# Moving the residual adds of two projections and two sets of weight sums from VectorE to GpSimd in a transformer layer kernel

## The chip, the cores and the metric

The kernel runs on one core of a Trainium2 chip. A core has TensorE (PE) for matrix products, VectorE (DVE), ScalarE (ACT) and GpSimd (POOL) for elementwise work, and SyncE (SP), which in this kernel issues nearly all transfers. Each engine executes its own queue of instructions. The metric is the device time of one execution in microseconds. The kernel before took 2554.41 us, the median of three runs (2552.43 to 2555.48).

## What is computed

One layer on x (2048 x 1024): token mixing (sliding-window attention and a gated linear recurrence, whose outputs are concatenated and projected by w_out), cross-attention with 4 heads into 256 memory tokens, and a dense SwiGLU FFN, each with a norm before and after and a residual. Cut to what matters here:

```python
y = jnp.concatenate([ya, yh], axis=-1) @ w_out[l]
h = h + rms_norm(y, g_mix_post[l])
u = rms_norm(h, g_x_pre[l])
m = rms_norm(mem, g_mem[l])
y = cross_attention(u, m, wq_x[l], wk_x[l], wv_x[l], wo_x[l])
h = h + rms_norm(y, g_x_post[l])
u = rms_norm(h, g_ffn_pre[l])
y = (jax.nn.silu(u @ w_gate[l]) * (u @ w_up[l])) @ w_down[l]
h = h + rms_norm(y, g_ffn_post[l])
```

All is float32.

## The kernel before

**Folded weights.** `fold_cross` makes, for each head, the products of the query weights with the memory's keys and of the memory's values with the output weights. They are stored as two matrices of 1024 x 1024, `qk_d` and `vo_d`. The scores are then one product of the tokens with `qk_d`, and the attention's output one product of the probabilities with `vo_d`.

**Precision.** Each float32 operand is split into a high part (ScalarE, or GpSimd in early stages, L987 and L989) and a low part, the difference (VectorE, L990). A product is three matmuls: L1131 high x high, L1132 high x low of T, L1133 low of S x high. S are the stationary tiles of a block, made anew for each (`streamed`, 5 buffers), T the moving ones of 512 columns, which stay for a whole job.

**Seven products for eight.** From the out projection on, the work is a list of jobs (`jobs`): out projection, scores, values, two halves of gate and up, three parts of the down projection. Each job multiplies a matrix, cut into 2 x 2 blocks, with 8 blocks of 256 tokens (22 of hidden rows) by Strassen's scheme in Winograd's form, seven steps of 12 matmuls a block in place of eight (`seven`). This needs sums of the blocks of both operands. S's sums are formed by VectorE for each block (L1106). T's sums are chains of four adds and subtractions, which `combined` (L1027 on) makes one job ahead: it loads two operands into tiles, combines them in place (L1034), and stores the result to HBM (L1035 calls `store`, on SP's queue). Each chain is done in two halves, thus 8 adds of 128 x 1024 for a job. The sums of `w_out` are made during token mixing, those of query-key (`qk_s`) beside the out projection, those of value-output (`vo_s`) beside the scores, the FFN's later (L1465 to L1473). A tile of the sums has few buffers: `extra` one, the second tile is a `row` (12 buffers, shared with the blocks' rows) for `qk_s` and a gain's tile for `vo_s`.

**The blocks.** `mixed_block` is the out projection of 256 tokens. Its `out` adds two PSUM or SBUF parts to a row y and squares it (L1526 on VectorE or L1528 on ScalarE, then L1504 on ScalarE). Its `after` works beside the following block's steps, a piece a step (each `yield` ends one): the norm's factors (`rstds`, three small GpSimd instructions, L1515 to L1519), y times factor and gain on VectorE (L1557), y plus the residual x (L1558), and the store of y to `h1_d`; then, two steps on, the squares of the new y on ScalarE, its norm's factors, and 32 x 32 transposes by VectorE (L1398) with a store for the score stage. `score_block` takes the maximum of each head's scores on VectorE (L1588), scales it on GpSimd (L1590) and forms exponentials on ScalarE (L1592). `value_block` scales y (L1630), adds the residual (L1634), stores it, squares it, scales it for the FFN (L1643) and transposes it on TensorE (L1390).

**Order.** `phases` goes through the steps: TensorE's products of a step, then the S tiles needed two steps on, then one piece of every follow-up and of the sums, then a split of the next job's T. On each engine the order of instructions is set at build by a simulated timeline. `behind` pins what is traced inside it behind the last ScalarE and VectorE instructions that were traced before (L1033); the pin holds for instructions on those two engines. SP's queue holds loads and stores in one order; a store that waits for its tile holds up the loads behind it.

Of the kernel before, what the change touches and what calls it, by code (L numbers as in the profile page):

```python
# [15 lines left out]
ALU = mybir.AluOpType  # L16
# [32 lines left out]
class Layer:  # L49
# [942 lines left out]
    CHAIN = (5, 7, 6, 4)  # L992

    def resident(self, get, nk, key, dst, keep, sums):


# [27 lines left out]
                keep[key] = src  # L1024
            yield lambda a=a, b=b, t=t, o=o: split(a, b, t, o)

    def combined(self, get, nk, dst):  # L1027

        nc = self.nc
        halves = [(0, (nk + 1) // 2), ((nk + 1) // 2, nk)]  # L1030
        for a, b in halves:
            def put(key, t, o, op):
                with self.behind():  # L1033
                    nc.vector.tensor_tensor(t, t, o, op)  # L1034
                self.store(dst[self.CHAIN.index(key), :, a * 512:b * 512], t.rearrange("p k d -> p (k d)"))  # L1035

            for x, y, key in (((0, 1), (0, 0), 5), ((1, 1), (0, 1), 7), (None, (0, 0), 6), (None, (1, 0), 4)):
                if x:
                    t = get(0, *x, a, b - a)
                o = get(1, *y, a, b - a)  # L1040
                for _ in range(3):
                    yield
                if key == 4:
                    put(4, o, t, ALU.subtract)
                else:
                    put(key, t, o, ALU.add if key == 6 else ALU.subtract)
                yield
# [132 lines left out]
    def plain(self, S, T, nk, out, keep, kind):  # L1180
# [36 lines left out]
        yield  # L1217

    def phases(self, jobs, first, prologue=None):


# [193 lines left out]
            p = P if i else 64  # L1415
            self.load(d, self.I["w_out"][r:r + p * n, j * 512:(j + 1) * 512].rearrange("(k p) d -> p k d", p=p))

    def sums(self, name, src, nk, *tiles):

        dst = self.tc.dram_tile([4, P, nk * 512], F32, name=name)  # L1420

        def get(which, i, j, k0, n):
            t = tiles[which]().rearrange("p (k d) -> p k d", d=512)[:, :n]
            src(t, i, j, k0, n)
            return t

        return dst, lambda: self.combined(get, nk, dst)

    def token_sums(self, a, o, n):

# [10 lines left out]
    def jobs(self):  # L1441
        I = self.I

        def weights(src, r0, nk):
            return lambda t, i, j, k0, n: self.load(
                t, src[r0 + (i * nk + k0) * P:r0 + (i * nk + k0 + n) * P, j * 512:(j + 1) * 512]
                .rearrange("(k p) d -> p k d", p=P))

        def ffn_u(b):
            return lambda t, i, j, k0, n: self.load(  # L1450
                t, self.u_d[4 * i + k0:4 * i + k0 + n, :, b * TB + j * 512:b * TB + (j + 1) * 512]
                .rearrange("k p t -> p k t"))

        def kinds(blocks, n=0, last="p"):
            return [("p" if i < n else last if i == len(blocks) - 1 else "s",) + b for i, b in enumerate(blocks)]

        def sums(name, src, nk, other=None):
            return self.sums(name, src, nk, self.extra_tile, other or self.gain_tile)

        def in_turn(*what):  # L1460
            return lambda: itertools.chain.from_iterable(w() for w in what)

        qk, vo = weights(self.qk_d, 0, 4), weights(self.vo_d, 0, 4)
        down = [(weights(I["w_down"], f0 * P, nk), f0, nk) for f0, nk in ((0, 3), (6, 4), (14, 4))]
        qk_s, vo_s = sums("qk_s", qk, 4, self.row_tile), sums("vo_s", vo, 4)  # L1465
        u_s = sums("u_s", ffn_u(1), 4)
        self.u0_s = self.tc.dram_tile([4, P, 4 * 512], F32, name="u0_s")
        d_s = [sums(f"d_s{c}", src, nk) for c, (src, _, nk) in enumerate(down)]
        jobs = [(self.w_out, 4, kinds([self.mixed_block(n) for n in range(0, NT, 2)], 1), self.out_sums, {1: [qk_s[1]]}),
                (qk, 4, kinds([self.score_block(n) for n in range(0, NT, 2)]), qk_s[0], {1: [vo_s[1]]}),  # L1470
                (vo, 4, kinds([self.value_block(n) for n in range(0, NT, 2)]), vo_s[0], {})]
        for b in range(NB):
            beside = {2: [in_turn(*(d[1] for d in d_s))]} if b else {4: [u_s[1]]}  # L1473
            jobs.append((ffn_u(b), 4, kinds([blk for f in range(0, NFF, 2) for blk in self.hidden_blocks(b, f)], 0, "s"),
                         u_s[0] if b else self.u0_s, beside))
        for c, (src, f0, nk) in enumerate(down):
            jobs.append((src, nk, kinds([self.down_block(c, f0, nk, n) for n in range(0, NT, 2)], 0, "s"), d_s[c][0], {}))

        return jobs
# [59 lines left out]
    def mixed_block(self, n):  # L1539
        nc = self.nc  # L1540
        y, x, ss = {}, [], []

        def out(i, j, a, b):
            if not y:
                x.extend(self.rows_of(self.I["x"], n + r) for r in range(2))
                ss.append(self.small("q_s", 4))
                if not n:
                    self.g_mix_post = self.gain(self.I["g_mix_post"])
            if i not in y:
                y[i] = self.row_tile()  # L1550
            self.squared(y[i][:, j * 512:(j + 1) * 512], a, b, ss[0][:, 2 * i + j:2 * i + j + 1])

        def after():
            r = self.rstds(ss[0])
            s2 = self.small("q_s", 4)
            for i in range(2):
                nc.vector.scalar_tensor_tensor(y[i], y[i], r[:, i:i + 1], self.g_mix_post, ALU.mult, ALU.mult)  # L1557
                nc.vector.tensor_tensor(y[i], y[i], x[i], ALU.add)  # L1558
                self.store(self.h1_d[(n + i) * P:(n + i + 1) * P, :], y[i])
                yield  # L1560
            yield
            for i in range(2):
                self.mean_squares(y[i], i, s2)
                yield
            r = self.rstds(s2)
            nc.gpsimd.tensor_scalar(self.r_x[:, n:n + 2], r, 1.0, None, ALU.mult)
            yield
            for i in range(2):
                self.store_blocked(self.h1t_d[n + i], self.blocked(y[i], self.row_tile()))
                yield  # L1570

        return self.tokens(self.y_d, n), out, after, None
# [37 lines left out]
    def value_block(self, n):  # L1610
        nc = self.nc
        y, ss, u, o = {}, [], {}, {}

        def out(i, j, a, b):
            if not y:
                ss.append(self.small("q_s", 4))
            if i not in y:
                y[i] = self.row_tile()
                if n == 0 and len(y) == 1:
                    self.g_x_post = self.gain(self.I["g_x_post"])  # L1620
                    self.g_ffn_pre = self.extra_tile()
                    self.load(self.g_ffn_pre, self.I["g_ffn_pre"][0:1, :].broadcast_to([P, D]))
            self.squared(y[i][:, j * 512:(j + 1) * 512], a, b, ss[0][:, 2 * i + j:2 * i + j + 1])

        def after():
            r = self.rstds(ss[0])
            s2 = self.small("q_s", 4)
            x = [self.rows_of(self.h1_d, n + i) for i in range(2)]
            for i in range(2):
                nc.vector.scalar_tensor_tensor(y[i], y[i], r[:, i:i + 1], self.g_x_post, ALU.mult, ALU.mult)  # L1630
            yield
            yield
            for i in range(2):
                nc.vector.tensor_tensor(y[i], y[i], x[i], ALU.add)  # L1634
                self.store((self.out if n < NT - 2 else self.h2_d)[(n + i) * P:(n + i + 1) * P, :], y[i])
                yield
            for i in range(2):
                self.mean_squares(y[i], i, s2)
                yield
            r = self.rstds(s2)  # L1640
            yield
            for i in range(2):
                nc.vector.scalar_tensor_tensor(y[i], y[i], r[:, i:i + 1], self.g_ffn_pre, ALU.mult, ALU.mult)  # L1643
                yield
            for i in range(2):
                u[i] = self.transposed(y[i], y[i])
                self.store_transposed(self.u_d, n + i, u[i])
                if 4 <= n < 8:
                    o[i] = self.row_tile().rearrange("p (k t) -> p k t", k=KT)
                    self.load(o[i], self.u_d[:, :, (n - 4 + i) * P:(n - 3 + i) * P].rearrange("k p t -> p k t"))  # L1650
                yield
            if o:
                yield
                for i in range(2):
                    yield from self.token_sums(u[i], o[i], n - 4 + i)

        return self.blocks(self.pt_d, n), out, after, None

    def hidden_blocks(self, b, f):
# [131 lines left out]
```

## Time and profile before

| | us |
|---|---|
| median of three runs | 2554.41 |
| the profiled execution | 2550.01 |
| its span, first to last instruction | 2548.3 |
| residual rows of the out projection (L1557), first to last start | 800.8 to 946.1 |
| maxima of the scores (L1590), first to last start | 962.7 to 1099.5 |
| residual rows of the values (L1634), first to last start | 1132.8 to 1289.2 |

The profile lists, for each engine, when an instruction ran, what it waited for and who waited for it. A row such as "L990 DVE TENSOR_TENSOR S<-sum,S 128x512" names the line of the kernel, the engine, the operation, the tile written and the tiles read, and the shape (partitions x elements). Idle time of an engine is put down to whatever ended it. Some matmul records are missing from a trace, so counts of matmuls can be a few per cent low. The granted TensorE clock was 0.997 of full speed.

The moved instructions are those of L1558 (16 times, 805.5 to 953.7 us), L1634 (16 times, 1132.8 to 1289.2), and of L1034 those of `qk_s` (8 times, 811.3 to 893.0) and `vo_s` (8 times, 982.4 to 1054.1).

### The profile page before, as it was taken

To read this page: it belongs to the slowest core of one execution; us is meant where nothing else is said; L and a number is where in the kernel's file an instruction comes from. 1 tells how busy PE (TensorE), PEld (TensorE's weight loads), DVE (VectorE), ACT (ScalarE), POOL (GpSimd) and SP (SyncE) were. 2 spreads that over 40 slices of the span, in tenths; PEclk is the share of its full clock that TensorE was granted. 3 is DMA by queue.
4 is the path that set the end of the run, shared out by engine and by line. 5 is a ranking of instruction groups with operands and counts; after the bars stand their busy time and mean duration, and the time that the engine had idled before them with its cause. 6 is when DMAs were issued, how large, how long until landed. Compare 5 with 4: busy or idle time off the path is not lost.

```text
span 2548.3 us, 34324 instructions
## 1 busy us (share of the span) xinstructions
PE 2504.8 (98%) x12006; PEld 2092.8 (82%) x12006; DVE 1792.1 (70%) x2871; ACT 1261.6 (50%) x2635; POOL 364.6 (14%) x540
## 2 busy tenths in 40 slices
PE   9999999999999999999999999999999999999998
PEld 8878888877997778878878888888888888878886
DVE  8885488987556989988876555576566557574766
ACT  5553466655555566566753333353333335443543
POOL 4231234321311112102200000000000000000022
PEclk9999999999999999999999999999999999999999
DMA  6455655865887996867954522254465434564786
GB/s 201 146 165 178 192 154 170 230 204 146 259 292 275 316 335 189 274 206 226 333 200 146 177 91 87 74 203 148 160 210 195 144 117 159 180 188 106 228 177 151
DMA packets 387885, 486.33 MB, mean 191 GB/s; under 512 B 22272, under 2 KB 283392, under 8 KB 387712
## 3 DMA queue, kind: packets, MB, share of 16 engines
q1 hardware_dynamic: 381664, 462.12, 55.9%
q0 software_dynamic: 6048, 22.02, 5.0%
q8 instruction: 94, 1.54, 0.2%
q14 instruction: 79, 0.65, 0.1%
HBM read 317.34 MB, written 166.72 MB: 190 GB/s over the span
## 4 chain that ended last, share of the span: by engine, by line
PE 51%; DVE 2%; DMA 1%; issue 1%; ACT 1%; POOL 0%; SPq 0%; DVEq 0%; POOLq 0%; ACTq 0%
PE psm L1133 17%; PE psm L1131 17%; PE psm L1132 17%; DVE T L990 0%; DVE S L990 0%; ACT junk L1504 0%; PE pss L1390 0%; DMA out_dram<-row 0%; DMA row<-d_s 0%; DMA row<-in_w_down_dram 0%; DMA u_d<-row 0%; DMA sraw<-in_w_gate_dram 0%; DVE sum L1106 0%; ACT S L987 0%; ACT T L987 0%
## 5 line engine op out<-in xcount | busy, mean ns | idle before, releaser
L1131 PE MATMUL psm<-T,S 128*128 128x512 f32 x2680 | 1034.1, 390 | 13.3 <-ACT part L1146 7.2
L1132 PE MATMUL psm<-T,S 128*128 128x512 f32 x2680 | 1042.3, 390 | 4.0 <-DVE T L990 3.9
L1133 PE MATMUL psm<-T,S 128*128 128x512 f32 x2680 | 1029.4, 389 | 4.1 <-DVE S L990 4.1
L1131 PEld LDWEIGHTS psm<-T,S 128*128 128x128 f32 x2680 | 503.0, 188 | 125.9 <-ACT part L1146 11.9
L1132 PEld LDWEIGHTS psm<-T,S 128*128 128x128 f32 x2680 | 503.2, 188 | 110.5 <-DVE T L990 7.3
L1133 PEld LDWEIGHTS psm<-T,S 128*128 128x128 f32 x2680 | 503.1, 188 | 110.6 <-DVE S L990 6.3
L987 ACT ACTIVATE S<-sum 128x512 fp32r<-128x512 f32 (+1 forms) x370 | 224.0, 620 | 371.5 <-PE psm L1133 267.3
L990 DVE TENSOR_TENSOR S<-sraw,S 128x512 fp32r<-128x512 f32 (+1 forms) x315 | 211.5, 679 | 218.8 <-ACT S L987 215.8
L1146 ACT ACTIVATE part<-psm 128x512 f32<-128x512 f32 x285 | 168.6, 596 | 251.9 <-PE psm L1133 230.9
L990 DVE TENSOR_TENSOR S<-sum,S 128x512 fp32r<-128x512 f32 (+1 forms) x388 | 257.4, 673 | 42.1 <-ACT S L987 38.3
L987 ACT ACTIVATE S<-sraw 128x512 fp32r<-128x512 f32 (+1 forms) x300 | 184.7, 618 | 110.8 <-PE psm L1133 106.0
L1537 POOL DMA_DIRECT2D y_d<-row x16 | 14.1, 879 | 1077.9 <-DVE row L1721 1027.6
L990 DVE TENSOR_TENSOR T<-row,T 128x1024 fp32r<-128x1024 f32 (+1 forms) x112 | 131.0, 1183 | 30.2 <-ACT T L987 29.2
L157 PE MATMUL psg<-u,whi 128*128 128x512 f32 x320 | 128.3, 401 | 0.0
L158 PE MATMUL psg<-u,wlo 128*128 128x512 f32 x320 | 127.6, 399 | 0.0
L156 PE MATMUL psg<-u,whi 128*128 128x512 f32 x320 | 127.5, 399 | 0.0
L1504 ACT ACTIVATE junk<-row 128x512 f32<-128x512 f32 x160 | 99.6, 624 | 40.6 <-DVE row L1526 20.6
L987 ACT ACTIVATE T<-row 128x1024 fp32r<-128x1024 f32 (+1 forms) x112 | 113.3, 1031 | 7.5 <-DMA row<-d_s 4.3
L1672 DVE TENSOR_TENSOR row<-psm,part 128x512 f32<-128x512 f32 x66 | 43.7, 687 | 66.9 <-PE psm L1133 66.9
L1681 DVE TENSOR_TENSOR part<-psm,part 128x512 f32<-128x512 f32 x66 | 43.8, 687 | 60.1 <-PE psm L1133 59.8
L1721 DVE TENSOR_TENSOR row<-psm,part 128x512 f32<-128x512 f32 x72 | 49.1, 688 | 49.5 <-PE psm L1133 49.4
L814 ACT ACTIVATE S<-S,w_mn 128x256 f32<-128x256 f32 (+1 forms) x128 | 63.0, 496 | 29.6 <-DVE w_mn L810 29.2
(363 smaller groups left out, 3562.2 us busy)
## 6 DMA issues: line engine op xcount, KB each, us to landing
sraw<-in_w_gate_dram SPq DMA_DIRECT2D x44, 512.0 KB, 3.6
sraw<-in_w_up_dram SPq DMA_DIRECT2D x44, 512.0 KB, 3.7
hid_d<-row SPq DMA_DIRECT2D x44, 512.0 KB, 2.7
sraw<-hid_d SPq DMA_DIRECT2D x32, 512.0 KB, 4.2
sraw<-in_w_in_dram SPq DMA_DIRECT2D x44, 256.0 KB, 4.0
z_d<-pair SPq DMA_DIRECT2D x20, 512.0 KB, 3.4
raw<-in_w_in_dram SPq DMA_DIRECT2D x20, 512.0 KB, 4.8
z_d<-z SPq DMA_DIRECT2D x20, 512.0 KB, 4.0
```

The source lines that it names most:

```text
L156: nc.tensor.matmul(ps, ah, bh, start=(i == 0), stop=False)
L157: nc.tensor.matmul(ps, ah, bl, start=False, stop=False)
L158: nc.tensor.matmul(ps, al, bh, start=False, stop=(i == n - 1))
L814: nc.scalar.activation(s[:, r, o:], s[:, r, o:], AF.Exp, bias=mn[:, i:i + 1], scale=-1.0, accum_out=den[:, i:i + 1])
L987: self.nc.scalar.activation(hi, raw, AF.Copy)
L990: self.nc.vector.tensor_tensor(lo, raw, f32(hi), ALU.subtract)
L1131: nc.tensor.matmul(ps, s[:, 0, k, :], t[:, 0, k, :], start=st, stop=False, **kw)
L1132: nc.tensor.matmul(ps, s[:, 0, k, :], t[:, 1, k, :], start=False, stop=False, **kw)
L1133: nc.tensor.matmul(ps, s[:, 1, k, :], t[:, 0, k, :], start=False, stop=sp, **kw)
L1146: nc.scalar.activation(t, ps, AF.Copy)
L1504: self.nc.scalar.activation(junk, a, AF.Square, scale=float(D) ** -0.5, accum_out=to)
L1721: nc.vector.tensor_tensor(d, a, b, ALU.add)
```

## The change

Two kinds of adds are issued on GpSimd in place of VectorE: the residual adds of `mixed_block` (L1558) and `value_block` (L1634), and the in-place adds of the sums `qk_s` and `vo_s` (L1034), through a new argument of `combined` and `sums`. The sums of `w_out`, of the FFN's tokens and of `w_down` stay on VectorE, as do all other instructions.

```diff
-    def combined(self, get, nk, dst):
-
-        nc = self.nc
+    def combined(self, get, nk, dst, on):
+
         halves = [(0, (nk + 1) // 2), ((nk + 1) // 2, nk)]
         for a, b in halves:
             def put(key, t, o, op):
                 with self.behind():
-                    nc.vector.tensor_tensor(t, t, o, op)
+                    on.tensor_tensor(t, t, o, op)
...
-    def sums(self, name, src, nk, *tiles):
+    def sums(self, name, src, nk, *tiles, on=None):
...
-        return dst, lambda: self.combined(get, nk, dst)
+        return dst, lambda: self.combined(get, nk, dst, on or self.nc.vector)
...
-        def sums(name, src, nk, other=None):
-            return self.sums(name, src, nk, self.extra_tile, other or self.gain_tile)
+        def sums(name, src, nk, other=None, **at):
+            return self.sums(name, src, nk, self.extra_tile, other or self.gain_tile, **at)
...
-        qk_s, vo_s = sums("qk_s", qk, 4, self.row_tile), sums("vo_s", vo, 4)
+        qk_s, vo_s = sums("qk_s", qk, 4, self.row_tile, on=self.nc.gpsimd), sums("vo_s", vo, 4, on=self.nc.gpsimd)
...
                 nc.vector.scalar_tensor_tensor(y[i], y[i], r[:, i:i + 1], self.g_mix_post, ALU.mult, ALU.mult)
-                nc.vector.tensor_tensor(y[i], y[i], x[i], ALU.add)
+                nc.gpsimd.tensor_tensor(y[i], y[i], x[i], ALU.add)
                 self.store(self.h1_d[(n + i) * P:(n + i + 1) * P, :], y[i])
...
             for i in range(2):
-                nc.vector.tensor_tensor(y[i], y[i], x[i], ALU.add)
+                nc.gpsimd.tensor_tensor(y[i], y[i], x[i], ALU.add)
                 self.store((self.out if n < NT - 2 else self.h2_d)[(n + i) * P:(n + i + 1) * P, :], y[i])
```

## The prediction

> **What bounds the kernel now.** I read the page's engine shares first, then the busy time by stretches, then who kept TensorE waiting, then single stretches of VectorE and GpSimd in order of time.
>
> ```profile
> span 2548.3 us, 34324 instructions
> PE 2504.8 (98%) x12006; PEld 2092.8 (82%) x12006; DVE 1792.1 (70%) x2871; ACT 1261.6 (50%) x2635; POOL 364.6 (14%) x540
> ```
>
> TensorE is the bound over the whole span: 2548.3 - 2504.8 = 43.5 us are all that can be gained anywhere. The edits lie in the three stages with folded cross-attention weights: out projection, scores, values. Here is the busy time of these (rows one to three) and of the following FFN stretch (row four):
>
> ```profile
> core 0: us, PE busy (x) PEld busy (x) DVE busy (x) ACT busy (x) POOL busy (x), PEclk, DMA share, GB/s
> 800.00:960.00 160.00, 153.24 (x666) 124.04 (x665) 143.69 (x184) 99.44 (x220) 25.61 (x50) 1.00 0.92 309
> 960.00:1120.00 160.00, 158.73 (x700) 130.90 (x699) 150.42 (x276) 99.35 (x227) 27.38 (x36) 1.00 0.77 235
> 1120.00:1320.00 200.00, 193.25 (x901) 157.24 (x900) 165.45 (x208) 128.59 (x275) 31.91 (x48) 1.00 0.76 251
> 1320.00:1700.00 380.00, 380.00 (x1678) 314.75 (x1677) 220.24 (x329) 144.25 (x249) 0.00 (x0) 1.00 0.39 129
> ```
>
> TensorE idles 6.76 us in the first stage, 1.27 in the second and 6.75 in the third, 14.8 in all; nothing in the FFN stretch. VectorE is busy 90%, 94% and 83% there. GpSimd is almost free by this count. Who ended TensorE's waits between 780 and 1320 us (sum, times, longest):
>
> ```profile
> PE psm L1133 <- DVE S L990: 4.1, 4, 1.6
> PE psm L1131 <- ACT S L987: 3.9, 3, 1.7
> PE psm L1132 <- DVE T L990: 3.9, 6, 1.4
> PE psm L1131 <- ACT part L1146: 2.4, 4, 1.3
> PE psm L1131 <- DVE row L1526: 0.3, 1, 0.3
> ```
>
> So 8.3 us are VectorE being late with the low halves of S and T, the rest ScalarE. ScalarE executes in order and waits for VectorE itself, so some of its part goes back to VectorE too. All that can be won by a less loaded VectorE is within these 14.8 us.
>
> **What is moved.** Groups of VectorE between 780 and 1320 us:
>
> ```profile
> L1558 DVE TENSOR_TENSOR row<-row,row 128x1024 f32<-128x1024 f32 x16 | 19.1, 1216 | 0.0
> L1634 DVE TENSOR_TENSOR row<-row,row 128x1024 f32<-128x1024 f32 x16 | 19.1, 1217 | 0.0
> L1034 DVE TENSOR_TENSOR extra<-extra,g 128x1024 f32<-128x1024 f32 x6 | 7.3, 1216 | 3.3 <-DMA extra<-vo_d 3.3
> L1034 DVE TENSOR_TENSOR extra<-extra,row 128x1024 f32<-128x1024 f32 x6 | 7.3, 1213 | 3.0 <-issue 1.9 <-DMA qk_s<-extra 1.1
> L1034 DVE TENSOR_TENSOR row<-row,extra 128x1024 f32<-128x1024 f32 x2 | 2.4, 1216 | 0.0
> L1034 DVE TENSOR_TENSOR g<-g,extra 128x1024 f32<-128x1024 f32 x2 | 2.4, 1215 | 1.2 <-DMA g<-vo_d 1.2
> ```
>
> 48 adds of 128x1024 go to GpSimd: 16 residual adds and 8 sums of query-key in the first stage, 8 sums of value-output in the second, 16 residual adds in the third. Nothing else is added or removed; loads and stores stay on SP. What an add costs VectorE is its start-to-start step, from this stretch of a block of the first stage:
>
> ```profile
> 866.57 2.47 DVE L1557 SCALAR_TENSOR_TENSOR row<-row,q_r,g 128x1024 f32<-128x1024 f32 x2
> 868.96 0.69 DVE L990 TENSOR_TENSOR S<-sraw,S 128x512 fp32r<-128x512 f32 x1
> 869.57 2.35 DVE L1558 TENSOR_TENSOR row<-row,row 128x1024 f32<-128x1024 f32 x2
> 871.84 0.68 DVE L990 TENSOR_TENSOR S<-sum,S 128x512 fp32r<-128x512 f32 x1
> 872.44 0.68 DVE L1526 TENSOR_TENSOR row<-psm,part 128x512 f32<-128x512 f32 x1
> 873.13 1.23 DVE L1034 TENSOR_TENSOR extra<-extra,row 128x1024 f32<-128x1024 f32 x1
> ```
>
> Two adds take 871.84 - 869.57 = 2.27, one 1.135 us. Freed: 24 x 1.135 = 27.2 us in the first stage, 9.1 in the second, 18.2 in the third.
>
> **What an add costs on GpSimd.** No GpSimd add of this shape is in the trace. Nearest are its two-input instructions with 256 and 512 elements (shortest/median/longest):
>
> ```profile
> L879 POOL TENSOR_TENSOR qq<-qq,G x16: 611/616/1378, 263.6 to 692.2; 128x256 f32<-128x256 f32 x16
> L891 POOL TENSOR_TENSOR q<-qq,G x16: 1042/1047/2197, 264.1 to 705.4; 128x512 f32<-128x512 f32 x16
> ```
>
> 256 more elements cost 1047 - 616 = 431 ns, so 1024 cost 1047 + 2 x 431 = 1.91 us (estimate). Bounds: VectorE's 1.22 below, twice the longest 512-element one, 4.39, above, which holds waiting as well. I take 1.91. That GpSimd is slower than VectorE by 0.7 us wouldn't matter by itself: in the code, two or three steps lie between a residual add and the squares that read its row.
>
> What matters is whether VectorE can work beside it. The longest cases hold the answer. Here are GpSimd's and VectorE's rows of one place and all instructions of L715:
>
> ```profile
> 410.63 1.04 POOL L914 TENSOR_TENSOR W<-W,G 128x512 f32<-128x512 f32 x1
> 411.63 1.49 POOL L891 TENSOR_TENSOR q<-qq,G 128x512 f32<-128x512 f32 x1
> 410.90 1.32 DVE L715 SCALAR_TENSOR_TENSOR z<-z,x 128x512 f32<-128x512 f32 x1
> L715 DVE SCALAR_TENSOR_TENSOR z<-z,x x8: 673/684/1320, 371.9 to 503.6; 128x512 f32<-128x512 f32 x8
> ```
>
> L715 reads two tiles of SBUF and normally takes 684 ns. Begun while GpSimd ran L914, it took 1320 and ended at 412.22, so its work began about 411.54, 0.91 us after L914 started. The next GpSimd instruction was then lengthened in turn by 0.44. The two engines exclude each other for nearly the whole instruction. Scaled, an add of 1.91 us keeps VectorE's two-input instructions out for 1.91 - 0.13 = 1.78 us.
>
> The Trainium skill ("SBUF — State Buffer", section "Who interferes with whom") states this as an exclusive lock: a VectorE instruction with two SBUF inputs and a GpSimd instruction that reads SBUF block each other for the whole instruction. The trace agrees, 1320 against 684 ns. The page "GPSIMD Engine Reference" (section 3.1) gives 4497 ns for a 2048-element add, half of which, 2.25 us (estimate), would make each add hold VectorE some 0.3 us longer than my rows do.
>
> VectorE instructions that read PSUM, or one SBUF tile, can run in the shadow. In the first stage these are mainly:
>
> ```profile
> L1398 DVE STREAM_TRANSPOSE row<-row 128x512 f32<-128x512 f32 x31 | 19.6, 679 | 0.0
> L1526 DVE TENSOR_TENSOR row<-psm,part 128x512 f32<-128x512 f32 x18 | 12.3, 682 | 1.9 <-ACT part L1146 0.9 <-DMA h1t_d<-row 0.9
> ```
>
> That is 31.9 us of the 143.69 - 27.2 = 116.5 that remain, 27%. Per add, VectorE loses between -1.135 us (never kept out) and 1.78 - 1.135 = +0.645 (kept out throughout); in the mean of the mix 0.73 x 1.78 - 1.135 = +0.165.
>
> **The sum.** First stage: 24 adds at +0.165 are 4.0 us, at +0.645 15.5. They come in bunches: both rows of a block and one sum within some 7 us, with S's low halves queued between them. So I take the middle, 9.7 us of VectorE's time, and half of it on TensorE, since VectorE idles 10% there: +4.9. Second stage: VectorE's own balance is 8 x 0.165 = 1.3 us, which its 6% of idle time takes up; but the sums now stand in GpSimd's queue ahead of the score maxima, for which ScalarE waits in order, and the first L1557 of a block waits for GpSimd's norms:
>
> ```profile
> ACT row L1592 <- POOL x_mr L1590: 25.2, 14, 6.4
> DVE row L1557 <- POOL q_r L1519: 2.7, 3, 1.2
> ```
>
> Each of 8 sums can push a maximum back by 0 to 1.91 us; TensorE idles only 1.27 us there although ScalarE already waits 25.2, so most is covered; I take 0.3 each, +2.4. Without that cover it is 15.3. Third stage: 17% idle on VectorE covers 16 x 0.165 = 2.6 us; I take 0, at most 10.3. Credit: a sum no longer stops VectorE while it waits for its transfer.
>
> ```profile
> 881.41 1.22 DVE L1034 TENSOR_TENSOR extra<-extra,row 128x1024 f32<-128x1024 f32 x1 [1.08 <-DMA qk_s<-extra]
> 883.15 0.68 DVE L990 TENSOR_TENSOR S<-sraw,S 128x512 fp32r<-128x512 f32 x1
> 883.89 0.50 PE L1133 MATMUL psm<-T,S 128*128 128x512 f32 x1 [1.25 <-DVE S L990]
> ```
>
> Here 1.08 us of waiting and the add stood right ahead of an S for which TensorE waited 1.25 us; this gap goes, and I give another 0.4 for the 1.9 us of the same group above that stand as issue: -1.7. The wait moves to GpSimd's queue, ahead of norms and maxima. SP's stores behind an add come at least 0.7 us later; SP loses more waiting for free buffers anyway (next rows), so I cost it at 0, or, without that cover, 0.7 x 48 = 34 us of a queue that is not the bound.
>
> ```profile
> SPq L75 <- DVE S L990: 439.2, 84, 13.6
> SPq L78 <- DVE row L1558: 27.3, 14, 6.1
> ```
>
> 4.9 + 2.4 - 1.7 = +5.6 us. The profiled execution took 2550.01 us, 1.7 around its span of 2548.3, and is 4.4 below the median of the three runs, 2554.41. Against the median: 2560.0 us. The kernel's engine orders are laid out anew at build from simulated times, and the order pin of a sum holds back VectorE and ScalarE instructions only, so a sum may also move in order; I allow 3 us either way for this.
>
> **Rivals.** *Faster.* GpSimd's adds fall into VectorE's idle time and its one-input instructions, 16 of 160 us plus 31.9 in the first stage, and VectorE's queue becomes short. For it: TensorE's 6.76 us of idle time in the first stage lie beside a VectorE that is 90% busy, and over half of all its waits name VectorE. Against: of three moved adds of a block two follow each other, so the shadow is used up. If the first stage's 6.8 us go and half of the 3.9 us for T, 1.9: 2554.4 - 8.7 = 2545.7. *Much slower.* GpSimd becomes a second queue on the path: each add starts when its row is ready, takes the read path at once, and the low half of an S always stands behind it; from two bunched adds on (3.6 us) a step of 12 matmuls, 12 x 380 / 1678 = 2.7 us by the FFN row, can't hide it. All 48 x 0.645 = 31 us, two thirds of it on TensorE: +20.6, 2575. Against it: VectorE and GpSimd took turns at 411, so S gets in between two adds. *No change.* The lock costs what the offload frees (0.165 a time), TensorE's slack holds both: 2554. For it: TensorE lost only 1.27 us with VectorE at 94%.
>
> By the skill's lock rule the "much slower" case is the natural end if GpSimd always starts first.
>
> **Chances.** My forecast, slightly slower, 0.44, with its own range 2551 to 2568; faster 0.31; much slower 0.15; no change 0.10. A measurement of this kernel can tell about 0.2%, 5 us, from no change. Faster by more: 0.30 of the faster case and 0.01 of mine; within: 0.01, the no-change 0.10 and 0.13 of mine; slower: 0.30 of mine and 0.15. That makes 0.31, 0.24, 0.45. Range 2544 to 2577: from the faster rival's 2545.7 to the much slower one's 2575, each with 2 us of spread.
>
> **What would show it.** Right: GpSimd adds near 1.9 us, many of them longer from waiting; S low halves of 128x512 (now 0.68) with some near 1.3 to 2.4 us; VectorE's busy time hardly smaller than before in the first stage although 24 instructions are gone; TensorE's idle time there 8 to 13 us. Faster: VectorE under 80% there and TensorE's idle under 3 us. Much slower: TensorE waiting for S low halves once or more a block, or for exponentials behind the maxima. Wrong altogether: time gained or lost outside 780 to 1320 us, which would be the new order and not the adds.

## The result, and the profile after

The kernel after takes 2599.45 us (median of 5 runs, 2598.09 to 2602.34) against 2554.41 (5 runs, 2552.43 to 2555.48): 1.0182 times as long, 95% interval 1.0171 to 1.0194. It is slower by 45 us, where 5.6 were forecast and 2577 was the end of the range. The profiled execution is the one of 2599.45 us, 49.4 above that of before.

The page of the kernel after, span and engine shares:

```profile
span 2597.7 us, 34341 instructions
PE 2521.9 (97%) x12006; PEld 2103.2 (81%) x12006; DVE 1827.6 (70%) x2823; ACT 1259.1 (48%) x2635; POOL 506.5 (19%) x588
```

VectorE has 48 instructions fewer and is busy 35.5 us longer (1827.6 against 1792.1). The 48 adds should have left 54.5 us with it (48 x 1.135).

Busy time by stretches of the kernel after, in the columns shown for before:

```profile
800.00:960.00 160.00, 143.21 (x590) 113.57 (x589) 138.57 (x134) 82.05 (x186) 87.76 (x67) 0.95 0.79 259
960.00:1120.00 160.00, 149.16 (x629) 120.72 (x628) 145.72 (x239) 90.90 (x214) 52.11 (x49) 0.97 0.74 227
1120.00:1320.00 200.00, 186.63 (x846) 151.71 (x845) 167.36 (x196) 119.16 (x264) 75.91 (x60) 0.98 0.74 237
1320.00:1700.00 380.00, 376.76 (x1669) 311.28 (x1668) 231.90 (x334) 152.67 (x270) 13.26 (x8) 1.00 0.41 134
```

Two things are to be seen. TensorE's idle time is 16.8 + 10.8 + 13.4 + 3.2 = 44.2 us, before 14.8: 29.4 more. And the granted clock, 1.00 in each of these rows before, is 0.95, 0.97 and 0.98: 0.05 x 160 + 0.03 x 160 + 0.02 x 200 = 16.8 us of work at full speed that weren't done. Together 46.2 of the 49.4; another 2.3 were lost ahead of 780 us, where nothing was changed. (The third stage now ends behind 1320, the last moved add starts at 1339.6.) What ended TensorE's waits from 780 to 1345 us (sum, times, longest; the smaller groups left out):

```profile
PE psm L1132 <- DVE S L990: 12.6, 6, 5.4
PE psm L1130 <- ACT S L987: 8.5, 5, 4.7
PE psm L1130 <- ACT part L1145: 7.4, 4, 2.9
PE pss L1389 <- DVE row L1642: 6.6, 3, 4.7
PE psm L1131 <- DVE T L990: 4.7, 4, 2.8
```

Low halves (L990) end 17.3 us of them; the rest ends with other rows of VectorE and with ScalarE.

Line numbers above 1026 are lower by one in the kernel after: its L1557 is the residual add, L1556 the scaling ahead of it, L1525 and L1105 are before's L1526 and L1106. In the other runs lines shift by a few more. The lengthened instructions, by groups of 780 to 1345 us of the kernel after (busy time, mean ns):

```profile
L990 DVE TENSOR_TENSOR S<-sraw,S 128x512 fp32r<-128x512 f32 x75 | 85.8, 1153 | 7.3 <-ACT S L987 7.3
L990 DVE TENSOR_TENSOR S<-sum,S 128x512 fp32r<-128x512 f32 x86 | 78.5, 915 | 19.6 <-ACT S L987 19.5
L990 DVE TENSOR_TENSOR T<-row,T 128x1024 fp32r<-128x1024 f32 x54 | 74.0, 1386 | 18.9 <-ACT T L987 18.9
```

The same groups before:

```profile
L990 DVE TENSOR_TENSOR T<-row,T 128x1024 fp32r<-128x1024 f32 x56 | 67.4, 1215 | 18.8 <-ACT T L987 17.8 <-DMA pt_d<-row 0.6
L990 DVE TENSOR_TENSOR S<-sum,S 128x512 fp32r<-128x512 f32 x96 | 64.7, 679 | 13.5 <-ACT S L987 13.3
L990 DVE TENSOR_TENSOR S<-sraw,S 128x512 fp32r<-128x512 f32 x84 | 57.2, 683 | 19.3 <-ACT S L987 19.3
```

75 x 0.470 + 86 x 0.236 + 54 x 0.171 = 64.8 us more in the low halves alone. The moved adds themselves (shortest/median/longest) and, below them, the low halves over the whole span:

```profile
L1557 POOL TENSOR_TENSOR row<-row,row x16: 2809/3370/3386, 806.1 to 973.3; 128x1024 f32<-128x1024 f32 x16
L1633 POOL TENSOR_TENSOR row<-row,row x16: 2407/3110/6593, 1168.2 to 1339.6; 128x1024 f32<-128x1024 f32 x16
L1033 POOL TENSOR_TENSOR extra<-extra,row x6: 2370/2607/2685, 798.7 to 896.5; 128x1024 f32<-128x1024 f32 x6
...
L990 DVE TENSOR_TENSOR S<-sraw,S x315: 551/691/2896, 11.7 to 2575.1; 128x512 fp32r<-128x512 f32 x146, 128x384 fp32r<-128x384 f32 x12
```

No add is shorter than 2.37 us, and a low half takes up to 2.90 in place of 0.69: it is kept out, that is, held up until the add has ended, for up to 2.2 us.

One place in order of time, first stage of the kernel after:

```profile
858.15 2.48 DVE L1556 SCALAR_TENSOR_TENSOR row<-row,q_r,g 128x1024 f32<-128x1024 f32 x2 [2.18 <-POOL q_r L1518]
859.51 3.37 POOL L1557 TENSOR_TENSOR row<-row,row 128x1024 f32<-128x1024 f32 x1 [1.40 <-DVE row L1556]
860.55 2.89 DVE L990 TENSOR_TENSOR S<-sraw,S 128x512 fp32r<-128x512 f32 x1
862.85 2.84 POOL L1557 TENSOR_TENSOR row<-row,row 128x1024 f32<-128x1024 f32 x1
863.36 2.88 DVE L990 TENSOR_TENSOR S<-sum,S 128x512 fp32r<-128x512 f32 x1
...
865.83 2.67 POOL L1033 TENSOR_TENSOR extra<-extra,row 128x1024 f32<-128x1024 f32 x1 [0.15 <-issue]
866.27 2.78 DVE L1105 TENSOR_TENSOR sum<-sraw 128x512 f32<-128x512 f32 x1
...
868.97 0.68 DVE L1525 TENSOR_TENSOR row<-psm,part 128x512 f32<-128x512 f32 x1
869.57 0.67 DVE L990 TENSOR_TENSOR S<-sum,S 128x512 fp32r<-128x512 f32 x1
...
871.63 0.50 PE L1130 MATMUL psm<-T,S 128*128 128x512 f32 x1 [2.76 <-DVE row L1525]
...
872.43 0.39 PE L1130 MATMUL psm<-T,S 128*128 128x512 f32 x1
872.65 0.59 PE L1131 MATMUL psm<-T,S 128*128 128x512 f32 x1
873.04 0.63 PE L1132 MATMUL psm<-T,S 128*128 128x512 f32 x1
...
875.60 0.63 PE L1132 MATMUL psm<-T,S 128*128 128x512 f32 x1
876.03 0.43 PE L1130 MATMUL psm<-T,S 128*128 128x512 f32 x1
876.30 0.39 PE L1131 MATMUL psm<-T,S 128*128 128x512 f32 x1
```

Each GpSimd add here catches the VectorE instruction that starts beside it, and the two take turns, as they did at 411 us before. Three adds in a row lengthen VectorE's instructions by 6.5 us ((2.89 - 0.68) + (2.88 - 0.68) + (2.78 - 0.68)). L1525, which reads TensorE's result out of PSUM and for which TensorE waits, stands behind all three, and TensorE stands still for 2.76 us. A microsecond after it resumes, a matmul starts every 0.43 us in place of 0.23, from 872.65 to 876.03: the clock is halved for 3.4 us, in which 1.7 us of work aren't done. So this gap is paid for twice.

### The profile page after: what moved, and what is told of

Same layout as the page of the kernel before. It is cut to its first block, busy times and chain, and to the rows that moved or that the text cites. A ratio compares the mean times of both kernels' runs of the same rounds, so it can differ in the third digit from the quotient of the medians.

```text
span 2597.7 us, 34341 instructions
## 1 busy us (share of the span) xinstructions
PE 2521.9 (97%) x12006; PEld 2103.2 (81%) x12006; DVE 1827.6 (70%) x2823; ACT 1259.1 (48%) x2635; POOL 506.5 (19%) x588
## 4 chain that ended last, share of the span: by engine, by line
PE 50%; DVE 5%; DMA 3%; issue 2%; ACT 2%; POOL 1%; SPq 1%; DVEq 0%; POOLq 0%; ACTq 0%
PE psm L1130 17%; PE psm L1131 17%; PE psm L1132 17%; DVE S L990 1%; DVE T L990 1%; ACT junk L1503 1%; DVE sum L1105 0%; SPq L78 0%; DMA row<-u_d 0%; PE pss L1389 0%; DMA row<-vo_d 0%; POOL row L1633 0%; DVE row L1397 0%; DMA row<-in_w_down_dram 0%; DMA vo_s<-extra 0%
## 5 line engine op out<-in xcount | busy, mean ns | idle before, releaser
L990 DVE TENSOR_TENSOR S<-sraw,S 128x512 fp32r<-128x512 f32 (+1 forms) x315 | 246.2, 791 | 214.8 <-ACT S L987 211.8
L990 DVE TENSOR_TENSOR S<-sum,S 128x512 fp32r<-128x512 f32 (+1 forms) x388 | 278.3, 726 | 50.7 <-ACT S L987 47.0
L990 DVE TENSOR_TENSOR T<-row,T 128x1024 fp32r<-128x1024 f32 (+1 forms) x112 | 140.2, 1267 | 31.8 <-ACT T L987 30.1
L1503 ACT ACTIVATE junk<-row 128x512 f32<-128x512 f32 x160 | 99.5, 623 | 81.8 <-DVE row L1525 60.1
```

The source lines that it names most:

```text
L990: self.nc.vector.tensor_tensor(lo, raw, f32(hi), ALU.subtract)
L1503: self.nc.scalar.activation(junk, a, AF.Square, scale=float(D) ** -0.5, accum_out=to)
```

## Experiments

Each kernel was timed against the kernel before on the same chip (2552.91 to 2554.5 us). The diffs are cut to their main lines; in the `beside` runs the eight adds of each of the two sums are treated like the rows. The table is worked out from the records of each profiled execution: the lengthening of VectorE's instructions against the usual duration of their form (780 to 1345 us: sum, count, longest), TensorE's gaps above 0.1 us (780 to 1400), its loss to the clock (half of the busy time at half clock), and gaps plus clock less the 14.8 of before, beside the measured difference.

```
                 lengthened us  count  longest | gaps  clock | more than  measured
                                                              before    difference
before                 0          0      0       14.8    0       0          0
after                 88.1       46     2.22     44.1   16.1   +45.4      +45.0
beside_add            73.3       39     2.21     52.8   18.7   +56.6      +60.1
beside_half           33.5       41     1.11     23.1    5.9   +14.2      +15.7
beside_read1          22.6       39     0.86     18.7    3.4    +7.3       +6.9
beside_memset          0.8        1     0.79     17.2    1.7    +4.1        0.0
left_out               0          0      0       11.8    1.7    -1.3       -6.5
pieces                46.8       95     0.62     38.1    8.7   +32.0      +31.7
p_rows_out            30.8       15     2.22     23.2    6.5   +14.9      +14.2
p_rows_val            32.2       15     2.21     24.5    4.4   +14.1      +13.4
p_sums                25.4       14     2.24     20.5    8.6   +14.3      +13.0
dma_add                0          0      0       37.5   12.3   +35.0      +33.8
dma_add_late           0          0      0       41.3   12.4   +38.9      +33.3
```

Gaps and clock give the measured difference within 6 us in every row. They stem from one profiled execution each, the differences from medians; beside_add's profiled execution, 65.6 us above that of before, exceeds its 56.6 by 9.

### Keeping out alone, GpSimd's occupation alone, and the adds left out

**beside_add**: VectorE keeps its adds, and GpSimd makes an idle one beside each.

```diff
+    def beside(self, y, used):
+        self.nc.gpsimd.tensor_tensor(used, used, y, ALU.add)
...
                 nc.vector.tensor_tensor(y[i], y[i], x[i], ALU.add)
+                self.beside(y[i], x[i])
```

> All 48 adds stay on VectorE as before; at the same 48 places GpSimd does one more add of 128x1024 that reads the fresh row and writes over the operand that is no longer needed, so nobody waits for its result. A (GpSimd's reads keep two-input VectorE instructions out): VectorE carries its 54.5 us of adds and some 88 us of being kept out, so more than the change itself: 2640 to 2680 us, S low halves of up to 2.9 us. B (rows, norms and maxima come later because they pass through GpSimd's slow queue): only norms and maxima are late, at most half of the change's 45 us, under 2577. C (another order of instructions): within 10 us of before.

2613.25 us, 1.0239 (1.0223 to 1.0254). Nobody waits for the results of these adds, nothing was taken from VectorE, and the loss is even larger: 60 us. The shape of the loss is that of the kernel after (longest stall 2.21 us, clock 0.95, 0.98 and 0.97 by stages). The time is 27 us below the lower end of what was expected.

**beside_memset** has in `beside` two memsets, which read nothing:

```diff
+        for _ in range(2):
+            self.nc.gpsimd.memset(used, 0.0)
```

> As the run with the extra adds, but GpSimd writes zeros twice over the operand that is no longer needed (some 2 us in all, no reading of SBUF). A: no VectorE instruction is lengthened, 2549 to 2560 us. B: GpSimd's queue is about as busy, so about the same time as with the extra adds.

2553.2 us, 1.0002 (0.9992 to 1.0011). One memset takes 0.96 us, so GpSimd is occupied for 1.9 us a place, and it costs nothing that can be measured:

```profile
L1484 POOL MEMSET row<- 128x1024 f32 x76 | 71.8, 956 | 96.8 <-DVE row L1640 42.3 <-DVE row L1563 37.8 <-DVE extra L1033 8.6
...
L990 DVE TENSOR_TENSOR S<-sum,S 128x512 fp32r<-128x512 f32 x90 | 60.9, 681 | 11.5 <-ACT S L987 11.4
```

The low halves of S keep their 681 ns. One instruction was lengthened, by 0.79 us: an L1606, a row scaled in place, that ran beside memsets. So a GpSimd queue fuller by 1.9 us a place isn't the cause of the loss; that its instructions read SBUF is. This is what the Trainium skill says ("SBUF — State Buffer", section "Who interferes with whom"): for a VectorE instruction with two SBUF inputs it excepts GpSimd instructions that only write.

**left_out**: the 48 adds are made by no engine, so rows lack their residual and sums their second operand. It shows what taking them off VectorE could win.

> The 48 adds are left out on both engines (no residual of the out projection and the values, operands of query-key and value-output not summed); all loads and stores stay. VectorE is freed of 54.5 us and GpSimd has nothing more to do. A and B: 2540 to 2552 us, the ceiling of what an offload could give. C: stays slower than 2580 because the order of the instructions is nearly that of the change.

2546.72 us, 0.9975 (0.9966 to 0.9985): 54.5 us less of VectorE's work are worth 6.5 us (3.8 to 8.7 by the interval).

### The three kinds of adds alone

After the change, two kinds at a time put back on VectorE. **p_rows_out** has only the residual rows of the out projection on GpSimd, **p_rows_val** only those of the values, **p_sums** only the sums.

```diff
-                nc.gpsimd.tensor_tensor(y[i], y[i], x[i], ALU.add)
+                nc.vector.tensor_tensor(y[i], y[i], x[i], ALU.add)
```

> Only the 16 residual adds of the out projection on GpSimd. A: a third of the adds in the stage with the busiest VectorE: 2565 to 2575 us. B: its squares and transposes wait for the rows: also 2565 or more.

> Only the 16 residual adds of the values on GpSimd, where VectorE idled 17% before. A: 2560 to 2572 us. B: as the out projection's.

> Only the 16 sums of query-key and value-output on GpSimd. A: as much per add as the rows, 2562 to 2572 us; the three parts together near 45 us. B: nobody waits soon for a sum, so within 5 us of before, and the two kinds of rows bear all of the 45 us.

2568.65 (1.0054, 1.0039 to 1.0069), 2567.91 (1.0052, 1.0036 to 1.0069) and 2567.48 us (1.0052, 1.0036 to 1.0068). All three are as their first expectations had them; only p_sums tells the two apart, since its second was within 5 us of before. 14.2 + 13.4 + 13.0 = 40.6 of the 45: nearly additive, 0.8 to 0.9 us an add, whether its result is awaited soon (rows) or a job later (sums). The 4.4 us that are left for the bunching of rows and sums lie within the intervals of these runs, each some 4 us to either side.

### How the cost grows with the length of a stall

**pieces**: the change, with each GpSimd add in four of 256 elements.

```diff
+    def pieces(self, d, a, b, op):
+        for c in range(0, D, 256):
+            self.nc.gpsimd.tensor_tensor(d[:, c:c + 256], a[:, c:c + 256], b[:, c:c + 256], op)
```

> The change with each of its GpSimd adds cut into four of 128x256. A: each piece keeps VectorE out for some 0.6 us and VectorE gets a turn in between; the sum of the kept-out time stays near 88 us but no single stall exceeds 1 us, so TensorE's gaps over 3 us and the clock's drops with them go: 2565 to 2590 us. B: the add takes longer from start to end, so slower than the change: over 2600.

2584.88 us, 1.0123 (1.0107 to 1.0139). VectorE gets in between the pieces: no instruction is kept out for more than 0.62 us, and 46.8 us of lengthening, where near 88 were expected, are less than the 54.5 freed. Yet 32 us are lost, inside the first expectation's range. The rows are late in another way now; groups and ScalarE's waits between 780 and 1345 us:

```profile
L1485 POOL TENSOR_TENSOR row<-row,row 128x256 f32<-128x256 f32 x128 | 153.8, 1237 | 33.1 <-DVE row L1636 13.9 <-DVE row L1563 10.3 <-DMA row<-h_d 5.2
```

```profile
ACT row L1598 <- POOL x_mr L1596: 46.1, 15, 6.9
...
ACT junk L1510 <- POOL row L1485: 14.5, 14, 2.0
```

A piece takes 1.24 us with its waiting, a row 4.9, and ScalarE waits 14.5 us for rows, 0.9 in the kernel before, and longer for the maxima, too. Two effects at once: this run doesn't tell what a short stall costs by itself.

So the length was changed where nobody waits for the result. **beside_read1** (`beside` copies the fresh row, one input: `tensor_scalar(used, y, 1.0, 1.0, ALU.mult, ALU.mult)`) and **beside_half** (the idle add over the first 512 elements alone: `tensor_tensor(used[:, :512], used[:, :512], y[:, :512], ALU.add)`).

> As the run with the extra adds beside VectorE's, but GpSimd copies the fresh row (one input of 1024 elements read in place of two). If the cost goes with the time for which GpSimd reads, each instruction keeps VectorE out for 0.9 us in place of 2.2, and of the extra adds' 60 us some 20 to 28 remain: 2573 to 2581 us. If it is only a matter of GpSimd's presence, as the extra adds, 2613.

> All adds stay on VectorE; at each of the 48 places GpSimd adds only the first 512 of the 1024 elements, again two inputs into an operand nobody reads any more. If the cost grows faster than the length of a stall, because a stall of about 1 us is mostly covered by the lead of the S tiles: some 40 to 48 VectorE instructions lengthened by about 0.9 to 1.1 us each, but only +5 to +20 us, 2559 to 2574. If each microsecond of keeping out costs the same: half of what the whole adds cost (60 us), +30, 2579 to 2589.

2561.04 us, 1.0028 (1.0017 to 1.0040), 12 us below the lowest time expected, and 2568.56, 1.0063 (1.0046 to 1.0079), as the first expectation had it. About 40 VectorE instructions were lengthened in all three, by at most 0.86, 1.11 and 2.21 us:

```profile
L990 DVE TENSOR_TENSOR S<-sraw,S x315: 550/691/1783, 11.8 to 2543.4; 128x512 fp32r<-128x512 f32 x146, 128x384 fp32r<-128x384 f32 x12
```

(beside_half; 1.78 at most). The time lost per microsecond of lengthening is 6.9 / 22.6 = 0.31, 15.7 / 33.5 = 0.47 and 60.1 / 73.3 = 0.82. So the price grows faster than the length. That the S tiles made ahead cover a short stall, and one of 2.2 us hardly, is an argument and wasn't traced. Nor does the length alone decide: the change and its three parts, with stalls as long (up to 2.24 us) but without the adds on VectorE, lost 0.42 to 0.51 per microsecond. The keeping out also occurs with a GpSimd instruction of a single input.

### A way round the lock

**dma_add**: the sums stay on VectorE, and the residual is added by an accumulating load that GpSimd issues, in place of the load of the residual row and the add; the squares come a step later, and the store just ahead of them.

```diff
-                nc.vector.tensor_tensor(y[i], y[i], x[i], ALU.add)
+                self.add(y[i], self.I["x"], n + i)
```

> Sums stay on VectorE; the 32 residual rows are added by accumulating transfers that GpSimd issues (the residual is added to the scaled row in SBUF while it is loaded), with the store and the squares a step or two later. If only GpSimd's reading of SBUF is what costs, VectorE is freed of 32 adds (36 us) at no cost to it, and the time comes two thirds of the way to the run without the adds: 2548 to 2552 us. If lateness of the rows or GpSimd's queue is what costs, it is slower than before, over 2560, since a landing takes some 8 us.

2588.0 us, 1.0135 (1.0118 to 1.0152): 36 us above the first expectation, inside the second. The keeping out is gone (no instruction lengthened) and VectorE is free (109.09 us of the first stage), but the rows land late and SP's stores, in order, wait for them:

```profile
800.00:960.00 160.00, 145.80 (x612) 117.70 (x612) 109.09 (x144) 85.50 (x188) 35.76 (x59) 0.96 0.91 257
```

```profile
SPq L78 <- DMA row<-in_x_dram: 55.2, 11, 16.6
```

**dma_add_late** moves the stores behind the squares, and these a step or two back.

> As the accumulating loads, with the stores of the residual rows and their squares moved back by one to two steps, so that SP's queue no longer stands behind a landing. If the ordered stores on SP made that version slow: SP's waits for the landed rows shrink from 73 us to under 15, and 2546 to 2556. If the lateness of what follows on GpSimd and ScalarE (issuing, factors of the norms, score maxima) made it slow: still over 2570, with ScalarE's wait for the maxima at 45 us or more.

2586.25 us, 1.0132 (1.0117 to 1.0147). The move didn't do what it was for, SP still waits for the landings, 83.8 us in all where under 15 were expected:

```profile
SPq L78 <- DMA row<-in_x_dram: 52.8, 13, 16.7
SPq L78 <- DMA row<-h_d: 31.0, 11, 4.6
```

Of the two expectations, neither fits whole: the time is the second's, but ScalarE waits for the maxima only 31.1 us, near the 25.2 of before. What would be left without SP's waits stays open, and so does a version faster than the kernel before; none was found.

## Why the prediction was wrong

The mechanism was named: the exclusion of the two engines, turns between them, low halves behind the adds, VectorE's busy time in the first stage hardly smaller (138.57 against 143.69), next to nothing lost outside these stages. Nearly all of its sizes were low, and they were put together in the wrong way.

**The add and its hold.** 1.91 and 1.78 us were scaled from rows of 256 and 512 elements; 2.37 us at the shortest and 2.2 were measured. The Trainium skill's "GPSIMD Engine Reference" (section 3.1), whose figure halved made an add 2.25 us (estimate), was nearer. With 2.2 the upper bound of an add is 2.2 - 1.135 = +1.07 us, not +0.645.

**The shadow.** The step that failed first is "in the mean of the mix 0.73 x 1.78 - 1.135 = +0.165". It took VectorE's instructions beside an add for a random draw, 27% of them harmless. They aren't random: a residual add is issued when the first L1556 of a block ends, waits while the second runs, and then holds up what stands behind the pair, mostly a low half (860.55 above). The prediction's own row at 868.96, right behind L1557 of before, shows the place. And what can run beside an add is over sooner than the add, so the next instruction is caught: at 888.70 an L1525 of 0.68 us kept its length, and the L990 behind it was held up by 1.6. 46 instructions were lengthened by 48 adds, 34 of them by 2 us or more, by 88.1 / 48 = 1.84 us an add; 33 of the 46 are low halves of S and T. The mean is +0.70 in place of +0.165.

**Balance against balance.** "Half of it on TensorE" weighed freed and lost time alike. The runs show that they differ: 54.5 us freed are worth 6.5 (left_out), 73.3 us lost in stalls of 2.2 us cost 60.1 (beside_add). A likely reason, not traced, is that freed time falls where TensorE has its S tiles anyway, and a stall right ahead of an S. The two runs give 60.1 - 6.5 = +53.6, the change +45.0. The difference isn't explained by a run: with its own adds still in the queue, VectorE has less to catch up with in beside_add, but this was only argued.

**The clock.** It had no term, and no reason was given for that. It makes 16 of the 45 us.

**Second stage.** +2.4 was for the sums ahead of the maxima in GpSimd's queue. TensorE's idle time there went from 1.27 to 10.84 us, and the clock to 0.97. Two gaps, 2.87 and 2.79 us, end at 968.05 and 977.27 with a part from ScalarE and a low half of T; that low half had been held up by a residual add. The third is the forecast case, and one gap of it is larger than the whole term:

```profile
1051.97 1.27 DVE L1587 TENSOR_REDUCE x_mx<-row 128x2 f32<-128x512 f32 x2
1053.27 2.80 POOL L1033 TENSOR_TENSOR extra<-extra,g 128x1024 f32<-128x1024 f32 x1 [5.37 <-DVE x_mx L1587]
1056.05 1.45 POOL L1589 TENSOR_SCALAR x_mr<-x_mx,r_x 128x2 f32<-128x2 f32 x2
1056.80 0.60 ACT L1591 ACTIVATE row<-row,x_mr,r_x 128x256 f32<-128x256 f32 x1 [6.06 <-POOL x_mr L1589]
1059.82 0.50 PE L1130 MATMUL psm<-T,S 128*128 128x512 f32 x1 [4.73 <-ACT S L987]
```

The maxima are ready at 1053.24, but their scaling (L1589) stands 2.8 us behind a sum's add; ScalarE waits for it, makes its exponentials, and only then the S for which TensorE has stood 4.73 us. ScalarE's wait for the maxima grew from 25.2 to 39.6 us between 960 and 1120 us. In beside_memset GpSimd was occupied, too (1.9 us a place), and nothing was lost, so the queue by itself doesn't explain the 45 us; how much of them passes through it no run tells apart, as the same add also kept an L1105 out.

**Third stage.** "I take 0, at most 10.3", because VectorE idles 17%. It cost 13.4 alone (p_rows_val). An average idle share doesn't cover a stall of 2.2 us at a fixed place.

**The credit** of 1.7 us is within what left_out won, 6.5; it wasn't measured by itself. **The order**: left_out and beside_memset were laid out anew, too, and lost nothing, so there is no sign that the new order is the cause.

**The rivals.** "Faster" fell, though its 8.7 us were a fair estimate of what freeing VectorE is worth (6.5). "Much slower" was the case that came true: two bunched adds that a step of 12 matmuls can't hide. Its reason against, that S gets in between two adds, holds at 860.55 and 863.36 and doesn't help, since what gets in has already waited for a whole add. Its price, 20.6 us, had 0.645 an add and no clock.

## What to carry to other kernels

Before an elementwise instruction that reads SBUF goes to GpSimd, look at which VectorE instruction follows at that very place, and charge it with the whole GpSimd instruction: where that one feeds TensorE, the offload costs more than it frees (here 1.84 against 1.135 us an add), however idle VectorE is on average. Don't net freed time against stalls: price the first with the work left out, the second with the work doubled beside it (the two came to 53.6 us for the 45 here). Where TensorE is the bound, give the clock a term of its own: 16 us here, beside 44 us of gaps.

## What the runs showed of the hardware

**The clock reacts to short gaps.** In the kernel before (longest wait 1.7 us) no piece of these stages ran at half clock. In the kernel after nine stretches did, of one or more pieces of 3.4 us, each with a gap of 1.8 to 5.4 us that begins in the 7 us ahead of it; in p_rows_out three stretches came behind gaps of at most 2.5 us. The length of one gap doesn't decide it: in beside_memset a gap of 1.72 us was followed by a half-clock stretch, the gap of 1.72 us in the kernel before by none. The Trainium skill ("TensorE: Matmul & The Clock Gate", section "Part 1") tells of an idle window of about 3.4 us; shorter gaps were enough here.

**GpSimd's instructions grow too.** L1557's median is 3.37 us against 2.37 for the shortest add: it waits for VectorE's instruction as VectorE waits for it. The turns aren't strict: the add at 1333.06 took 6.59 us, while five low halves in a row ran beside it at their usual length. What gave VectorE the way there stays open.

**An accumulating load isn't a free add.** Its rows landed some 8 us after issue (medians 7.7 and 8.1 in dma_add, 8.5 and 8.4 in dma_add_late), where VectorE's add takes 1.2.
